# Input products of the state-space branch one projection later, and the pooling branch's running sums on GpSimd

## The chip, the cores and the metric

The kernel runs on one core of a Trainium2 chip. The metric is the device time of one execution in microseconds (us); less is better. The program of one core has five engines with an instruction queue each: TensorE (PE in the profile), VectorE (DVE), ScalarE (ACT), GpSimd (POOL) and SyncE (SP), which here issues the DMAs. An engine starts its instructions in the order of its queue; engines wait for each other by semaphores.

## The reference, cut to what matters

The reference is a network of two blocks on 512 tokens of 1024 channels in fp32. The change lies in the second block, whose first product is split into six parts; two branches work on them:

```python
h = _rmsnorm(x, norm_g[l])
proj = h @ w_in[l] + b_in[l]
ua, za, ub, zb, ga, gb = jnp.split(proj, SPLITS, axis=-1)
ya = _s5_branch(ua, ...) * jax.nn.silu(za)
yb = _pool_branch(ub, pool_w[l], pool_scale[l]) * jax.nn.silu(zb)
merged = jax.nn.sigmoid(ga) * (ya @ w_branch_a[l]) + jax.nn.sigmoid(gb) * (yb @ w_branch_b[l])
x = x + merged @ w_out[l]

def _s5_branch(u, ...):                 # 32 groups of 16 channels
    bu_re = jnp.einsum('blgc,gpc->blgp', ug, bbar_re)      # input products
    bu_im = jnp.einsum('blgc,gpc->blgp', ug, bbar_im)
    _, _, s_re, s_im = lax.associative_scan(_complex_linear_combine, (a_re, a_im, bu_re, bu_im), axis=1)
    y = einsum(s_re, c_re) - einsum(s_im, c_im) + d_skip * u
    ...

def _pool_branch(u, w_group, scale):    # 4 groups of 128 channels, a window for each
    mean = (csg - shifted) / count      # mean of the last `win` tokens
    outs.append(mean - u32[group])
    ...
    return einsum(pooled, w_group) * scale
```

## The kernel before

Tokens lie on the free axis: a tile is 128 channels by 512 tokens. A projection (`proj`) is one such tile: 24 matmuls of 128x512 into a PSUM tile `psp`, three (leading by leading, remaining by leading, leading by remaining parts of fp32 values, L264 to L266) for each of eight 128-channel slices k0 to k7, then one ScalarE instruction that adds the bias and applies the function. `chunk` calls a hook after each slice, so other matmuls can be put between the slices. Weights come as blocks of 128x1024 by DMA (`r_win`), one block for a projection here; ScalarE makes the leading part (`h_win`, L245) and VectorE the remaining part (`l_win`, L246).

The second block's projections come in this order, with what stands between them: ua0 to ua3; ub0, zb0, ub1, zb1, the pooling product out0, ub2, zb2, out1, ub3, zb3, za0, za1, out2, za2, out3, za3; then the gates. TensorE's order is written out by hand (`manual_schedule`); the order of the other engines is set by a scheduler from the program and its dependencies.

The state-space branch is a generator, `ssm_main`, that the program advances by `next(ssm)` or hands to `proj` as the hook. It loads tables, the input weights `wi` and the input `U` (written by ua0 to ua3 to DRAM and read back by eight DMAs, L1652). Then come the input products `pb`: eight groups of eight matmuls of 128x64 (L1658) in two halves each, with a step of the hook behind each half, and the copies to `BR` and `BI` on ScalarE (L1662, L1663). Behind the last of them VectorE runs a chain of 16 instructions: six products of `cmul` (L1371 to L1376) and two scans (L1668), four more products (L1672, L1673), four that write `XR` and `XI` (L1676). This chain is called the chain below. Two of the four output weight tiles `wo` reuse the chain's scratch buffers `bt0` and `bt1`, so their DMAs (L1681) wait for its end; the output products `py` (L1692, L1693) stand as the hook in za2 and za3 and need the first `wo` tile, `XR` and `XI`. With nine `yield`s in front of the input products, zb1's hook runs the eight groups.

The pooling branch is `pool_proj` (ub and zb), `pool_mix` (on VectorE: the running sum by doublings, 1 to 4 of them (L1732, each with a small copy, L1733), the product with the reciprocal counts `rcn` (L1736), the difference (L1737), then the split of the mean into `ybh` on ScalarE, L260, and `ybl` on VectorE, L261) and `pool_out` (three matmuls, scale and gate `ybf`, L1746, split again).

Of the kernel before, what the change touches and what calls it, by code (L numbers as in the profile page):

```python
# [11 lines left out]
AF = mybir.ActivationFunctionType  # L12
ALU = mybir.AluOpType
# [23 lines left out]
# x1 projections of the hyena mixer by the quarter of the channels that they follow  # L37
# [18 lines left out]
def host_inputs(inp):  # L56
# [68 lines left out]
    def both(a):  # L125
        # states on partitions twice, groups on the free axis; halves of the groups on partitions
        a = a.reshape(2, 16, 64)
        st = a.reshape(32, 64).T
        return np.concatenate([np.concatenate([st, st], axis=0), a.transpose(0, 2, 1).reshape(128, 16)], axis=1)
# [64 lines left out]
def build(nc, tc, A, dbg=None):  # L194
# [36 lines left out]
    class Stream:  # L231
        """128x128 weight units in blocks of eight, split into leading and remaining significand parts"""
# [85 lines left out]
    def residual_gemm(pp, ws, acts, evac, u_of=lambda m: m * 8, klead=2, nhalf=2, nxt=None, norm=None, at={}, bg=None, pss=None):  # L318
        if nhalf:
            nhalf, sk = NHS[ncall[0]], SKS[ncall[0]]  # L320
            ncall[0] += 1
        if callable(acts):
            n = KT
        else:
            n, acts = len(acts), acts.__getitem__

        def done(m, sl, ps):
            evac(m, sl, ps)
            if norm is not None:
                norm.add(m, sl)  # L330
            if bg is not None:
                bg(m)

        if pss is not None:
            klead = len(pss)
        else:
            pss = [pp.tile([128, L], F32, name="ps_r", tag="mm") for _ in range(klead)]
            for k in range(n):
                if k in at:
                    at[k]()  # L340
                for m in range(klead):
                    mm3(pss[m], ws.unit(u_of(m) + k), acts(k), k == 0, k == n - 1)
        acts = [acts(k) for k in range(n)]
        for m in range(klead):
            done(m, FULL, pss[m])
        if callable(pp):
            pp = pp()
        for m in range(klead, KT - nhalf):
            ps = pp.tile([128, L], F32, name="ps_r", tag="mm")
            chunk(ps, ws, u_of(m), acts, FULL)  # L350
            done(m, FULL, ps)
        if not nhalf:
            return
        if nxt is not None:
            for b in range(u_of(KT - nhalf) // 8, (u_of(KT - 1) + n - 1) // 8 + 1):
                ws.load(b)
            for b in range(3):
                nxt.load(b)
        # the table of the coming square roots, out of the way of the norm
        tc.keep_in_program_order(act.activation(dummy, epst, AF.Sqrt))  # L360
        for i, sl in enumerate(norm.parts):
            for m in range(KT - nhalf, KT):
                ps = pp.tile([128, L], F32, name="ps_r", tag="mm")[:, :sl.stop - sl.start]
                if i == 1 and m == KT - nhalf:
                    chunk(ps, ws, u_of(m), acts, sl, at_steps({sk[0]: lambda: norm.stat(0), sk[1]: lambda: norm.spread(0)} if norm.hook() is None else {2: lambda: norm.stat(0)}))
                else:
                    chunk(ps, ws, u_of(m), acts, sl, norm.hook() if i == 1 and m == KT - 1 else None)
                done(m, sl, ps)
        if norm.hook() is None:
            norm.apply(0)  # L370

# [26 lines left out]
    # leading and remaining parts of both vectors as four stationary columns  # L398
# [27 lines left out]
    def range_sin(tp, out, a, shape, quarter=False, tag=""):  # L426
        """out = sin(a) (cos(a) if quarter) of an unbounded argument"""
# [18 lines left out]
    def hyena_filter(hp, tp, pp, t):  # L446
# [19 lines left out]
        # the layer's leading and remaining parts over each other: both times the weights' leading parts in one pass  # L466
# [33 lines left out]
        def spectrum(qd, m, ta):  # L500
            s = 1 - m
            # sums and differences of the residue classes (cosine parts for the sum sequence, sine for the other)
# [72 lines left out]
    def mod_cols(hf, nr, scr):  # L575
        """rows to columns, with the bias; gains of the norms"""
        pst = pp.tile([128, 16], F32, name="pst0", tag="mm")
        for n in range(8):
            pe.matmul(pst[:, 2 * n:2 * n + 2], scr[n // 4][:, (n % 4) * 128:(n % 4 + 1) * 128], sel if nr == 4 else ident[0:2, 0:2], start=True, stop=True)
        pv = pst.rearrange("p (j n s) -> p j s n", j=2, s=2)  # L580
        o = slice(4 * hf, 4 * hf + 4)
        for s_, g in ((0, gM0), (1, gC0)):
            d = scc[:, 8 * s_ + 4 * hf:8 * s_ + 4 * hf + 4]
            dve.tensor_tensor(out=d, in0=pv[:, 1, s_], in1=V("modb", 8 + 4 * hf, 4), op=ALU.add)
            gain(g[:, o], d, V("nmix", 4 * hf, 4))
        for s_, dst in ((0, mods[:, o]), (1, shc[:, o])):
            dve.tensor_tensor(out=dst, in0=pv[:, 0, s_], in1=V("modb", 4 * hf, 4), op=ALU.add)
# [21 lines left out]
    def rstat_of(acc, dim, ps=None):  # L609
        """1/rms over the channels, on the tokens' partitions"""  # L610
# [9 lines left out]
    def rspread(sd, ps=None, out=None):  # L620
        """back to the free axis, the same on every partition"""
# [278 lines left out]
    # the queries' norm goes with the rotary table, token by token  # L900
# [27 lines left out]
    def osplit(k):  # L928
        """remaining parts in place of the previous head pair's values"""
# [5 lines left out]
    def wo_lead():  # L935
        """first output tiles, as far as the heads are done"""
# [87 lines left out]
    class Norm:  # L1024
        """rms norm of the residual stream: statistics as its tiles get ready, use in halves of the tokens"""
# [25 lines left out]
        def stat(self, i):  # L1051
            """on the tokens' partitions"""
# [20 lines left out]
        def spread(self, i):  # L1073
            """back to the free axis, the same on every partition"""
# [122 lines left out]
    up = Stream(A["wup"][1], "up1")  # L1197

    def hyena(ws, hh, hl, pre, norm, nxt):
# [15 lines left out]
        # convolution constants: interior bias, corrections at the two ends  # L1215
# [19 lines left out]
        def fft(q, vh, vl):  # L1235
            """transform, product with the filter's spectrum and inverse butterflies of 256 channels"""
            hf, cs = q // 2, slice((q % 2) * W, (q % 2) * W + W)
            # pairs of real and imaginary parts; (im, re) where they are combined crosswise
# [145 lines left out]
    def ssm_prep(ph):  # L1384
        """weights of the state-space branch for chunks of T steps"""
# [5 lines left out]
        # columns of the small tables: all groups, states' real parts over imaginary ones; then halves of the groups  # L1391
# [4 lines left out]
        # imaginary parts have the opposite sign on the lower half of the stacked tables  # L1396
# [21 lines left out]
        # powers of the transition  # L1418
# [19 lines left out]
        # input coefficient times the powers, for steps that lie 0..7 before the chunk's last  # L1438
# [9 lines left out]
        # the skip connection is a diagonal part of the kernel's tap of lag zero (its rows are the last sixteen)  # L1448
# [13 lines left out]
        def weights(name, q, a, b, x, op):  # L1462
            """a x + b y or a x - b y of complex numbers, real parts over imaginary ones"""
# [16 lines left out]
        for q in range(4):  # L1480
            gs = slice(8 * q, 8 * q + 8)
            # kernel taps
# [13 lines left out]
            # input weights, transposed  # L1496
# [12 lines left out]
            # output weights: real part and negated imaginary part of C abar^(t+1)  # L1509
# [12 lines left out]
        # conjugate powers of the phasor of T steps, decay of T steps  # L1522
# [34 lines left out]
    # final norm of the first block and the second block's norm in one pass over the statistics  # L1557
# [4 lines left out]
    # 1/rms of the once normed stream, without the first norm's factor: the sum of squares of x sqrt(g^2 + eps)  # L1562
# [74 lines left out]
    def ssm_main(pa):  # L1637
# [15 lines left out]
        for _ in range(9):  # L1653
            yield
# [14 lines left out]
        # back to the states' own phase: multiply by the conjugate table; real over imaginary parts  # L1669
# [47 lines left out]
    def pool_proj(gi, hook=None):  # L1717
# [3 lines left out]
        proj(12 + gi, AF.Silu, zb, hook)  # L1721
        ubz[gi] = (ub, zb)

    def pool_mix(gi):
# [4 lines left out]
        for s in range(gi + 1):  # L1729
            w = 1 << s  # L1730
            nxt = tmp("cum")
            dve.tensor_tensor(out=nxt[:, w:], in0=run[:, w:], in1=run[:, :L - w], op=ALU.add)  # L1732
            dve.tensor_copy(nxt[:, :w], run[:, :w])  # L1733
            run = nxt
        mean = tmp("mean")
        dve.tensor_tensor(out=mean, in0=run, in1=rcn, op=ALU.mult)  # L1736
        dve.tensor_tensor(out=mean, in0=mean, in1=ub, op=ALU.subtract)  # L1737
# [18 lines left out]
    pool_proj(1, ssm)  # L1756
    pool_out(0)
    pool_mix(1)
    next(ssm)
    pool_proj(2)  # L1760
# [36 lines left out]
    # gated linear unit of the state-space branch  # L1797
# [23 lines left out]
    # gated sum of the branches  # L1821
# [25 lines left out]
    class Final(Norm):  # L1847
        """last norm: tokens to the partitions, where the statistics scale them"""
# [84 lines left out]
```

## Time and profile before

| | us |
|---|---|
| median of 3 runs | 1738.53 |
| lowest and highest | 1736.77, 1740.84 |
| span of the profiled execution | 1744.6 |
| PE busy in it | 1718.7 (99%) |
| DVE busy | 1223.3 (70%) |
| ACT busy | 840.1 (48%) |
| POOL busy | 0.7 (0%), 9 instructions |

The profiled execution is 6.1 us longer than the median. Sums are made on its own times, and their difference is laid on the median. "Busy" counts an engine's instructions, not its waits. A busy PE may run at a lower clock: the column PEclk of the views by stretch is the granted TensorE clock, 1.00 for 2.4 GHz and 0.50 for 1.2 GHz.

### The profile page before, as it was taken

The page shows a single profiled execution, that of the slowest core. Times are in us where ns is not written, and L with a number is a line of the kernel's source. Part 1 is how long each engine was busy: PE and PEld are TensorE (multiplying, and loading weights), DVE is VectorE, ACT ScalarE, POOL GpSimd, SP SyncE. Part 2 cuts the span into 40 slices and gives each one's busy share as a digit, 9 for nine tenths or more (in the row PEclk, how much of TensorE's full clock was granted, in tenths as well). Part 3 has the DMA queues.
Part 4 walks back from the last instruction along what each step waited for, and adds up shares of the span by engine and source line. Part 5 has one row for each costly group of instructions (what it writes and reads, how often), then busy time and mean ns, then how long its engine had stood idle before and what let it go on. Part 6 is the DMA issues. An engine that isn't in the chain of part 4 may idle for free.

```text
span 1744.6 us, 22561 instructions
## 1 busy us (share of the span) xinstructions
PE 1718.7 (99%) x8645; PEld 1427.1 (82%) x8645; DVE 1223.3 (70%) x2065; ACT 840.1 (48%) x1299; POOL 0.7 (0%) x9
## 2 busy tenths in 40 slices
PE   8999999999999999999999999999999999999998
PEld 2678888887988888888888898888888898888887
DVE  5666999884799875654899969884586452927443
ACT  4566889995544313433533355442244243345234
POOL 0000000000000000000000000000000000000000
PEclk8989999999999999999999999999999997999999
DMA  6533432111478773222332332444542246443221
GB/s 226 185 132 115 139 109 91 37 37 61 153 237 270 266 244 109 97 99 84 122 105 97 113 109 79 146 138 150 141 145 97 97 166 143 150 116 121 97 85 49
DMA packets 91862, 224.87 MB, mean 129 GB/s; under 512 B 22728, under 2 KB 38344, under 8 KB 91626
## 3 DMA queue, kind: packets, MB, share of 16 engines
q1 hardware_dynamic: 91754, 223.42, 38.8%
q8 instruction: 68, 1.11, 0.3%
q14 instruction: 40, 0.33, 0.1%
HBM read 206.64 MB, written 16.74 MB: 128 GB/s over the span
## 4 chain that ended last, share of the span: by engine, by line
PE 90%; DVE 5%; ACT 2%; DMA 1%; issue 1%; SPq 0%; DVEq 0%
PE ps_r L264 7%; PE ps_r L265 7%; PE ps_r L266 7%; PE psg L266 4%; PE psg L265 4%; PE psg L264 4%; PE psa L266 4%; PE psa L264 4%; PE psa L265 4%; PE psp L264 3%; PE psp L265 3%; PE psp L266 3%; PE pac L498 2%; PE pst L880 2%; PE pso L891 1%
## 5 line engine op out<-in xcount | busy, mean ns | idle before, releaser
L245 ACT ACTIVATE h_up<-r_up 128x1024 fp32r<-128x1024 f32 x88 | 92.9, 1056 | 146.9 <-PE psg L265 81.3
L264 PE MATMUL ps_r<-mh,h_dn 128*128 128x512 f32 (+1 forms) x407 | 148.5, 365 | 0.0
L265 PE MATMUL ps_r<-ml,h_dn 128*128 128x512 f32 (+1 forms) x407 | 148.3, 364 | 0.0
L266 PE MATMUL ps_r<-mh,l_dn 128*128 128x512 f32 (+1 forms) x407 | 148.3, 364 | 0.0
L246 DVE TENSOR_TENSOR l_up<-r_up,h_up 128x1024 fp32r<-128x1024 f32 x88 | 107.4, 1220 | 52.0 <-ACT h_up L245 47.3
L266 PE MATMUL psg<-hh,l_up 128*128 128x512 f32 x336 | 132.9, 396 | 0.0
L265 PE MATMUL psg<-hl,h_up 128*128 128x512 f32 x336 | 131.7, 392 | 0.0
L264 PE MATMUL psg<-hh,h_up 128*128 128x512 f32 x336 | 131.5, 391 | 0.0
L266 PE MATMUL psa<-hh,l_up 128*128 128x512 f32 x320 | 125.9, 394 | 0.0
L265 PE MATMUL psa<-hl,h_up 128*128 128x512 f32 x320 | 124.6, 389 | 0.0
L264 PE MATMUL psa<-hh,h_up 128*128 128x512 f32 x320 | 124.5, 389 | 0.0
L386 DVE CUSTOM_DVE_ANT_0 mr<-mr,cb 128x1024 f32<-128x1024 f32 x80 | 97.0, 1218 | 23.1 <-DMA mr<-modT 22.4
L245 ACT ACTIVATE h_dn<-r_dn 128x1024 fp32r<-128x1024 f32 x44 | 46.5, 1057 | 105.4 <-PE ps_r L265 65.1
L264 PE MATMUL psp<-hh,h_win 128*128 128x512 f32 x232 | 94.5, 407 | 0.0
L265 PE MATMUL psp<-hl,h_win 128*128 128x512 f32 x232 | 91.8, 396 | 0.0
L266 PE MATMUL psp<-hh,l_win 128*128 128x512 f32 x232 | 91.8, 396 | 0.0
L246 DVE TENSOR_TENSOR l_dn<-r_dn,h_dn 128x1024 fp32r<-128x1024 f32 x44 | 53.6, 1221 | 49.6 <-ACT h_dn L245 49.6
L265 PEld LDWEIGHTS ps_r<-ml,h_dn 128*128 128x128 f32 x407 | 76.5, 188 | 13.6
L264 PEld LDWEIGHTS ps_r<-mh,h_dn 128*128 128x128 f32 x407 | 76.5, 188 | 13.6
L266 PEld LDWEIGHTS ps_r<-mh,l_dn 128*128 128x128 f32 x407 | 76.5, 188 | 13.6
L246 DVE TENSOR_TENSOR l_win<-r_win,h_win 128x1024 fp32r<-128x1024 f32 x32 | 39.0, 1223 | 67.9 <-ACT h_win L245 67.7
L1156 ACT ACTIVATE og<-og 128x512 f32<-128x512 f32 x44 | 27.8, 631 | 111.8 <-DVE og L1113 110.1
(663 smaller groups left out, 4598.4 us busy)
## 6 DMA issues: line engine op xcount, KB each, us to landing
r_up<-wup SPq DMA_DIRECT2D x88, 512.0 KB, 3.7
mr<-modT SPq DMA_DIRECT2D x80, 512.0 KB, 4.3
r_dn<-wdn SPq DMA_DIRECT2D x44, 512.0 KB, 3.7
r_win<-win SPq DMA_DIRECT2D x32, 512.0 KB, 3.4
r_hyin<-hyin SPq DMA_DIRECT2D x24, 512.0 KB, 3.3
rmod<-mod SPq DMA_DIRECT2D x8, 512.0 KB, 6.6
x<-xT SPq DMA_DIRECT2D x16, 256.0 KB, 4.8
Hd<-ho SPq DMA_DIRECT2D x16, 256.0 KB, 2.3
```

Of the source, the lines that this page charges most:

```text
L245: act.activation(hi, raw, AF.Copy)
L246: dve.tensor_tensor(out=lo, in0=raw, in1=hi.bitcast(F32), op=ALU.subtract)
L264: pe.matmul(ps, w[0], a[0], start=start, stop=False)
L265: pe.matmul(ps, w[0], a[1], start=False, stop=False)
L266: pe.matmul(ps, w[1], a[0], start=False, stop=stop)
L386: dve.tensor_tensor_reduce(raw, raw, cb, 1.0, 0.0, ALU.mult, ALU.add, mods[:, n:n + 1])
L498: pe.matmul(ps, tabs[:, o * 128:(o + 1) * 128], ta[r], start=(i == 0), stop=(i == len(terms) - 1))
L880: pe.transpose(pst[:, i * 128:(i + 1) * 128], Pt[h, i][:, j * 128:(j + 1) * 128], ident)
L891: pe.matmul(Ot[h], vw, pth, start=(j == 0), stop=False)
L1156: act.activation(og, og, AF.Silu)
```

## The change

Comment lines that only went away are left out. `ssm_main` yields once instead of nine times before the input products; `zb` projections no longer run the hook, and the hook goes with projection ub2 instead of ub1 and zb1. The running sums, their small copies, the product with `rcn` and the difference go from VectorE to GpSimd: 18 instructions of 128 by about 512 and 10 small copies (3 and 1 in the first mix, 4 and 2, 5 and 3, 6 and 4 in the others). The split of the mean stays on ScalarE and VectorE. Lines behind L1653 have a number less by one afterwards.

```diff
@@ ssm_main
-        for _ in range(9):
-            yield
+        yield
         for q in range(4):
             pb = pp.tile([128, 8, NJ], F32, name="pb", tag="bg", bufs=2)
@@ pool_proj
         proj(8 + gi, AF.Identity, ub, hook)
-        proj(12 + gi, AF.Silu, zb, hook)
+        proj(12 + gi, AF.Silu, zb)
@@ pool_mix
             nxt = tmp("cum")
-            dve.tensor_tensor(out=nxt[:, w:], in0=run[:, w:], in1=run[:, :L - w], op=ALU.add)
-            dve.tensor_copy(nxt[:, :w], run[:, :w])
+            nc.gpsimd.tensor_tensor(out=nxt[:, w:], in0=run[:, w:], in1=run[:, :L - w], op=ALU.add)
+            nc.gpsimd.tensor_copy(nxt[:, :w], run[:, :w])
             run = nxt
         mean = tmp("mean")
-        dve.tensor_tensor(out=mean, in0=run, in1=rcn, op=ALU.mult)
-        dve.tensor_tensor(out=mean, in0=mean, in1=ub, op=ALU.subtract)
+        nc.gpsimd.tensor_tensor(out=mean, in0=run, in1=rcn, op=ALU.mult)
+        nc.gpsimd.tensor_tensor(out=mean, in0=mean, in1=ub, op=ALU.subtract)
@@ order of the second block
     pool_mix(0)
-    pool_proj(1, ssm)
+    pool_proj(1)
     pool_out(0)
     pool_mix(1)
+    pool_proj(2, ssm)
     next(ssm)
-    pool_proj(2)
     next(ssm)
     pool_out(1)
```

On TensorE, before, the input products stand in projection zb1 (weight block 7), from behind its first slice on:

```order
L264 MATMUL psp<-hh_9545,h_win_7_13129 128x512
L265 MATMUL psp<-hl_9553,h_win_7_13129 128x512
L266 MATMUL psp<-hh_9545,l_win_7_13130 128x512
L1658 MATMUL pb<-U,wi 128x64 x4
L264 MATMUL psp<-hh_9546,h_win_7_13129 128x512
L265 MATMUL psp<-hl_9554,h_win_7_13129 128x512
L266 MATMUL psp<-hh_9546,l_win_7_13130 128x512
L1658 MATMUL pb<-U,wi 128x64 x4
```

Now they stand in ub2 (weight block 8), behind zb1 and the three matmuls of out0 (`ybh_13010` and `pwl` are its last):

```order
L266 MATMUL psp<-ybh_13010,pwl 128x512
L264 MATMUL psp<-hh_9545,h_win_8_13161 128x512
L265 MATMUL psp<-hl_9553,h_win_8_13161 128x512
L266 MATMUL psp<-hh_9545,l_win_8_13162 128x512
L1657 MATMUL pb<-U,wi 128x64 x4
L264 MATMUL psp<-hh_9546,h_win_8_13161 128x512
L265 MATMUL psp<-hl_9554,h_win_8_13161 128x512
L266 MATMUL psp<-hh_9546,l_win_8_13162 128x512
L1657 MATMUL pb<-U,wi 128x64 x4
```

So the products ask for `U` one projection and out0 later in the program.

On VectorE, before, the beginning of the chain (`bt`, `XR`) stands between the instructions of the second mix (`ybl_13015` is its `ybl`):

```order
L1732 TENSOR_TENSOR cum<-ub 128x511
L1733 COPY cum<-ub 128x1
L1371 TENSOR_TENSOR bt_13257<-BR,TR__13023 128x1024
L261 TENSOR_TENSOR ybl_13014<-ybf,ybh_13010 128x512
L1732 TENSOR_TENSOR cum<-cum 128x510
L1733 COPY cum<-cum 128x2
L1372 TENSOR_TENSOR bt_13258<-BI,TI__13024 128x1024
L1736 TENSOR_TENSOR mean<-cum,rcn 128x512
L1373 TENSOR_TENSOR XR<-bt_13257,bt_13258 128x1024
L1737 TENSOR_TENSOR mean<-mean,ub 128x512
```

Now the second half of the chain on VectorE holds the `ybl` of the third and fourth mix (`ybl_13016`, `ybl_13017`), whose means GpSimd makes, and the remaining part of the weights of za2 (`l_win_14`) stands behind it:

```order
L1671 TENSOR_TENSOR bt_13323<-BR,TR__13023 128x1024
L1672 TENSOR_TENSOR bt_13324<-BI,TI__13024 128x1024
L261 TENSOR_TENSOR ybl_13015<-ybf,ybh_13011 128x512
L1675 TENSOR_TENSOR XR<-bt_13323,bt_13324 64x1024
L1675 TENSOR_TENSOR XI<-bt_13323,bt_13324 64x1024
L261 TENSOR_TENSOR ybl_13016<-mean,ybh_13012 128x512
L1671 TENSOR_TENSOR bt_13323<-BI,TR__13023 128x1024
L1672 TENSOR_TENSOR bt_13324<-BR,TI__13024 128x1024
L261 TENSOR_TENSOR ybl_13017<-mean,ybh_13013 128x512
L1675 TENSOR_TENSOR XR<-bt_13323,bt_13324 64x1024
L1675 TENSOR_TENSOR XI<-bt_13323,bt_13324 64x1024
L246 TENSOR_TENSOR l_win_14_13506<-r_win_14_13503,h_win_14_13505 128x1024
```

No running sum is left on VectorE there, and the chain's last instructions come after two that read what GpSimd writes.

On GpSimd, which had nine memsets, the fourth mix now reads:

```order
L1731 TENSOR_TENSOR cum<-ub 128x511
L1732 COPY cum<-ub 128x1
L1731 TENSOR_TENSOR cum<-cum 128x510
L1732 COPY cum<-cum 128x2
L1731 TENSOR_TENSOR cum<-cum 128x508
L1732 COPY cum<-cum 128x4
L1731 TENSOR_TENSOR cum<-cum 128x504
L1732 COPY cum<-cum 128x8
L1735 TENSOR_TENSOR mean<-cum,rcn 128x512
L1736 TENSOR_TENSOR mean<-mean,ub 128x512
```

It is the last of the four, which stand in GpSimd's queue one behind the other.

## Rows read from the trace of the kernel before

**Rows 1.** The page: its head and its first part, busy time by engine.

```profile
span 1744.6 us, 22561 instructions
PE 1718.7 (99%) x8645; PEld 1427.1 (82%) x8645; DVE 1223.3 (70%) x2065; ACT 840.1 (48%) x1299; POOL 0.7 (0%) x9
```

**Rows 2.** Waits of PE, 1440 to 1550 us: total us, times, longest.

```profile
PE pb L1658 <- DMA r_win<-win: 2.8, 1, 2.8
PE psp L264 <- ACT ybh L260: 1.1, 1, 1.1
```

**Rows 3.** By stretch: us; busy PE, PEld, DVE, ACT, POOL; PEclk, DMA share, GB/s.

```profile
1458.20:1461.10 2.90, 0.10 (x1) 0.00 (x0) 0.00 (x0) 0.14 (x1) 0.00 (x0) 0.98 1.04 299
1461.10:1482.70 21.60, 21.56 (x86) 19.67 (x86) 1.23 (x1) 5.44 (x8) 0.00 (x0) 0.53 0.17 65
1482.70:1489.10 6.40, 6.40 (x30) 5.29 (x30) 6.14 (x10) 2.94 (x6) 0.00 (x0) 1.00 0.26 87
1489.10:1516.80 27.70, 27.70 (x123) 22.73 (x122) 27.55 (x30) 6.78 (x9) 0.00 (x0) 1.00 0.37 126
1516.80:1519.40 2.60, 1.25 (x5) 0.67 (x4) 2.47 (x5) 1.21 (x2) 0.00 (x0) 1.00 0.97 254
```

**Rows 4.** PE in order of time: start, us, instruction, times, idle before and releaser.

```profile
1461.14 1.94 PE L1658 MATMUL pb<-U,wi 128*128 128x64 f32 x8 [2.84 <-DMA r_win<-win]
...
1481.85 1.00 PE L1658 MATMUL pb<-U,wi 128*128 128x64 f32 x8
1482.66 0.48 PE L264 MATMUL psp<-ybh,pwh 128*128 128x512 f32 x1
...
1520.10 0.33 PE L1692 MATMUL py<-U,wk 128*128 128x64 f32 x2
```

**Rows 5.** SP's DMA issues in order of time: start, us, line, transfer, times.

```profile
1447.09 7.54 SPq L1652 DMA_DIRECT2D U<-Ud  x8
...
1512.39 0.80 SPq L1681 DMA_DIRECT2D wo<-Wod  x2
```

**Rows 6.** DVE in order of time, 1485 to 1512 us: parts of the chain.

```profile
1485.43 1.22 DVE L1371 TENSOR_TENSOR bt<-BR,TR__13023 128x1024 f32<-128x1024 f32 x1
1486.56 0.69 DVE L261 TENSOR_TENSOR ybl<-ybf,ybh 128x512 fp32r<-128x512 f32 x1
1487.16 0.68 DVE L1732 TENSOR_TENSOR cum<-cum 128x510 f32<-128x510 f32 x1
...
1494.18 2.29 DVE L1668 TENSOR_TENSOR_SCAN BR<-R__13025,XR 128x1024 f32<-128x1024 f32 x1
...
1497.50 0.75 DVE L1746 SCALAR_TENSOR_TENSOR ybf<-psp,vecs,zb 128x512 f32<-128x512 f32 x1
...
1509.87 1.22 DVE L1676 TENSOR_TENSOR XR<-bt,bt 64x1024 f32<-64x1024 f32 x1
1511.11 1.22 DVE L1676 TENSOR_TENSOR XI<-bt,bt 64x1024 f32<-64x1024 f32 x1
```

**Rows 7.** DMA by transfer, 1505 to 1520 us: KB each, median us to landing.

```profile
wo<-Wod SPq DMA_DIRECT2D x4, 512.0 KB, 4.1
```

**Rows 8.** ACT in order of time, 1480 to 1490 us: one instruction.

```profile
1489.98 0.69 ACT L1621 ACTIVATE ub<-psp,vecs 128x512 f32<-128x512 f32 x1
```

**Rows 9.** POOL in order of time: two of its nine instructions.

```profile
0.73 0.21 POOL L217 MEMSET ones<- 128x128 f32 x1 [0.29 <-POOLq L1923]
0.87 0.10 POOL L218 MEMSET epst<- 128x1 f32 x1
```

**Rows 10.** By stretch, columns as in rows 3, around two other stalls.

```profile
432.00:434.00 2.00, 0.20 (x1) 0.20 (x2) 0.90 (x2) 1.00 (x2) 0.00 (x0) 1.00 0.00 0
434.00:436.00 2.00, 2.00 (x9) 1.52 (x9) 1.18 (x2) 0.94 (x1) 0.00 (x0) 1.00 0.00 0
...
164.00:166.00 2.00, 0.96 (x8) 0.72 (x6) 1.34 (x3) 0.86 (x2) 0.00 (x0) 1.00 0.30 88
168.00:170.00 2.00, 2.00 (x11) 2.00 (x11) 1.72 (x5) 1.09 (x4) 0.00 (x0) 0.50 0.82 315
```

## The prediction

> **What bounds the kernel now.** I read the page first: PE is busy for 1718.7 of 1744.6 us, DVE for 1223.3 and POOL for 0.7 [rows 1], so a change pays only where PE waits or runs slowly. The view of PE's waits between 1440 and 1550 us names two that matter: 2.8 us of the input products pb, and 1.1 us of out2 for ybh [rows 2]. The first stall is larger than its own length. The view by stretch [rows 3] has PE idle from 1458.2 to 1461.1, and then 21.6 us at a granted clock of 0.53, nearly all of it at the lower of the two levels (1.2 GHz), although PE has work all the time; from 1482.7 on it is 1.00 again. The releaser printed for pb is the DMA of r_win, but that is only the transfer that came last by the profile; pb reads U, whose eight DMAs take 7.54 us to issue, until 1454.6 [rows 5], and the matmul that waits is pb's [rows 4]. I take U as the cause.
>
> Behind that, DVE is the engine to watch: from 1489.1 to 1516.8 us it is busy for 27.55 of 27.70 [rows 3], with the chain between the running sums [rows 6]. Out2 and py come right behind it: py starts at 1520.10 [rows 4].
>
> **Part 1, the products one projection later: PE's side.** Costs at the full clock: 123 matmuls of 128x512 in 27.70 us [rows 3] are 0.225 each, so a projection is 5.4 and a pooling product 0.7. Eight pb matmuls take 0.81, from 1481.85 to the next start at 1482.66 [rows 4], so all 64 take 6.5, and a projection with them 11.9.
>
> In the new order PE goes on at 1458.2 with the 21 matmuls left of zb1 (4.7, to 1462.9), out0 (to 1463.6) and ub2 with pb (11.9, to 1475.5). pb asks for U at 1464.3, some 3 us after it was there before (1461.14, [rows 4]); the same DMAs stand in the same place of SP's queue, ahead of r_win, with only the load of rcn moved up behind them. So this wait is gone. With it goes the low clock: 21.6 us were 11.9 of work, 9.7 lost. Ub2 ends at 1475.5 instead of 1489.1: PE is 13.6 us earlier. The five projections and out1 behind it (27.70) end at 1503.2; out2 and the first slice of za2 need 0.7 each, so py is reached at 1504.6 if nothing waits.
>
> **The chain's side.** It started 2.77 us after pb's end (1482.66 to 1485.43, [rows 4, 6]); now pb ends at 1475.5, so it starts at 1478.3, only 7.2 earlier, because the products were put later by what the stall had cost. Its length, from start to start: a product 1.13 and a split 0.60 (1485.43, 1486.56, 1487.16), a scan 2.20 (2.29 with the same overlap of 0.09), XR or XI 1.24 [rows 6]. Ten products, two scans and four of these make 11.3 + 4.4 + 5.0 = 20.7. By the new order three ybl (1.8) and one ybf (0.7) stand among them: 23.2 of DVE's own. Alone, it ends at 1501.5; the wo transfers behind it were issued at 1512.39, right at its end (1511.11 + 1.22), and take 4.1 to land [rows 5 to 7], which gives 1505.6. That is 1.0 after PE asks, and 14.5 before 1520.10. This is the best the change can do: **−14.5**, with no slack.
>
> **Part 2, the sums on POOL: what they cost.** DVE is rid of 18 instructions of 128x512 at 0.60 and 10 copies, about 12 us, of which most lay in or near the chain; the 23.2 already has them out. What they take on POOL no row shows, since POOL runs nine memsets. Lower bound: the 0.69 that DVE takes for a split of this size [rows 6]. Upper bound: a memset of 128x128 holds POOL for 0.14 (0.73 to 0.87, [rows 9]), so 128x512 would be 0.56, and two reads and a write three times that, 1.7. I take the middle, 1.2; for a copy of 1 to 8 columns 0.1 (a memset of 128x1, [rows 9]) to 0.25, taken as 0.2.
>
> Mixes 0 and 1 are covered: the first has from ub0 to out0, some 13 us of PE's work, for 3.8, and the second has ub2 and zb2 for 5.2. Mix 2 can start when ub2 is evacuated, 1.6 after PE's end (1489.1 to 1489.98 + 0.69, [rows 3, 8]), at 1477.1, and mix 3 when ub3 is, at 1488.7. Both run beside the chain: 11 large and 7 small instructions, 11 x 1.2 + 7 x 0.2 = 14.6 us. If the engines don't disturb each other, mix 2 ends at 1483.7 and mix 3 at 1496.7, before the ybl that read them come up (the last one 3.1 before the chain's end, at 1498.4), and the chain waits for nothing; at 1.7 it would wait some 2.
>
> **The step that decides.** How much of these 14.6 us falls on the chain, by slower instructions or by waits, no row can tell, since DVE and POOL never work together before. The bounds are none and all; below none is excluded, as the chain's 23.2 can't shrink. What each amount D is worth: py is late by D over 1505.6, and PE's wait grows to 1.0 + D in all. A wait of 2.84 us was followed by the low clock [rows 4, 3], one of 1.8 us at 432 was not, and one around 165 was for some us only [rows 10]; out2's stop before (1.25 busy of 2.60, rows 3) did nothing to the clock either. So for D up to about 2 the gain stays at 12 or more; from about 2 on the low clock under the products py, which mix with projection matmuls as pb did, gives back up to 9.7. Only the lowest tenth or so of the possible D gives a faster kernel. I therefore take the far end, all of it: the two engines take turns, D = 14.6 + 0.6 (the ScalarE copy of the last mean, which the last ybl then waits for as well) = 15.2. The chain ends at 1516.7 and wo lands at 1520.8. Behind the chain in DVE's queue stands the l_win of za2, so PE waits in pieces: some 3 us before out2 (ybl of mix 2), and some 12 more between out2 and py.
>
> The Trainium skill, page "SBUF — State Buffer", section "SBUF: two separate sides", says that a VectorE instruction with two SBUF inputs and a GpSimd instruction that reads SBUF exclude each other for a whole instruction. No run here shows it yet; by it the sum is the one with turns, and without it the one of the best case. The page "GPSIMD Engine Reference", section 3.1, measured an add at 4497 ns on GpSimd against 2293 on VectorE; scaled from the 0.69 of this trace I estimate 1.35 a piece from it, which would make the turns 1.7 us longer.
>
> **Sum.** py at 1520.8 against 1520.10 is +0.7; the low clock costs +9.7, as in the stretch of 21.6. In sum +10.4: the profiled execution would be 1755.0, and since it is 6.1 above the median, the median **1748.9**. With 0.69 a piece and 0.1 a copy, D is 8.9: −14.5 + 8.9 + 9.7 = +4.1, 1742.6; with 1.7 and 0.25, D is 21.0: +16.2, 1754.7.
>
> **The rivals.**
> 1. *Not slower: the engines run side by side.* DVE's instructions of one kind have equal length whatever ACT and PE do beside them (1.22 at 1485 and 1511, [rows 6]), which speaks for it; that a two-operand instruction on POOL needs the same memory speaks against. D is 0 to 2, the clock stays: −14.5 to −12, 1724 to 1727. It decides up to D of 2. Chance 0.20.
> 2. *Partly disturbed:* D between 2 and 6, or turns with the clock kept. −12.5 to −8.5, with 9.7 given back or less; or +0.7 with no loss of clock. 1734 to 1742. Chance 0.13.
> 3. *Turns, and dearer:* POOL nearer 1.7, or the low clock through za2 and za3, which both carry py (two times 9.7 instead of one). 1738.5 + 0.7 + 19.4 = 1758.6; with both 1764. Chance 0.17.
> 4. *The change doesn't do what it says:* pb waits for U in its new place, or something else (the first instruction on POOL, late rcn) stops PE there for 3 us, so the low clock comes back at pb and what is won is lost. About 1738. Chance 0.03.
> The forecast, turns at 0.69 to 1.7 with one stretch of low clock, 1742 to 1755, has 0.47.
>
> **How the numbers follow.** About 0.2%, 3.5 us, is what a measurement of this kernel can tell from no change. Faster than 1735: rival 1 (0.20) and a third of rival 2 (0.04), 0.24. Within 1735 to 1742: the rest of rival 2, rival 4 and the edge of the forecast, 0.13. Slower: 0.63. The range reaches over the upper half of rival 1 and most of rival 3: 1726 to 1760.
>
> **What would show it.** In the profile after: no wait of pb and PEclk 1.00 in zb1, out0 and ub2 (part 1); the chain's start some 7 us earlier than 1485.43; POOL rows of 0.7 to 1.7 us for the large instructions; then, for the forecast, chain instructions or POOL instructions that are longer, or start later, where both engines work, an end of the chain at about 1517, waits of PE for ybl, l_win and wo of 15 us together, and a stretch of PEclk near 0.5 under py. I am wrong if the chain ends before about 1504, with instructions of 1.22 beside a busy POOL, or if PE waits long before py and its clock stays at 1.00.

## The result, and the profile after

The changed kernel took 1754.74 us (median of 5 runs, 1751.27 to 1766.60) where the kernel before took 1738.53 (median of 5 runs taken beside them, 1736.27 to 1743.80). The ratio is 1.0104, with a 95% interval of 1.0075 to 1.0133: slower by about 1%. The forecast was 1748.9, in a range of 1726 to 1760.

The page of the profiled execution (1766.6 us, the longest of the five): its head and its first part. The rows answer to [rows 1].

```profile
span 1764.7 us, 22576 instructions
PE 1734.4 (98%) x8645; PEld 1440.4 (82%) x8645; DVE 1218.7 (69%) x2037; ACT 839.2 (48%) x1299; POOL 37.9 (2%) x37
```

DVE's busy time fell by 4.6 us only, where 28 instructions less should take some 12 off it, and POOL's rose by 37.2, where the prediction had 24 (18 x 1.2 + 10 x 0.2). Both engines were busy longer than forecast.

PE's waits between 1440 and 1570 us (total, times, longest), which answer to [rows 2]:

```profile
PE psp L266 <- DVE l_win L246: 7.4, 1, 7.4
PE py L1692 <- DMA wo<-Wod: 1.4, 1, 1.4
```

Both waits of before are gone. pb no longer waits, and neither does out2. In their place PE waits 7.4 us for the l_win of za2 and 1.4 for the first wo, 8.8 in all where it was 4.1.

The same program by stretch, columns as in [rows 3]:

```profile
1458.20:1477.00 18.80, 18.80 (x118) 16.72 (x116) 4.56 (x6) 9.51 (x15) 4.92 (x6) 1.00 0.37 137
1477.00:1504.20 27.20, 27.20 (x122) 22.51 (x122) 26.74 (x17) 6.51 (x10) 23.81 (x16) 1.00 0.18 59
1504.20:1512.00 7.80, 2.13 (x10) 1.42 (x8) 4.62 (x5) 3.31 (x5) 4.24 (x3) 0.84 0.62 201
1512.00:1518.00 6.00, 2.87 (x10) 2.59 (x11) 5.21 (x6) 0.63 (x1) 0.00 (x0) 0.50 0.74 265
1518.00:1564.00 46.00, 46.00 (x169) 41.37 (x169) 6.24 (x7) 7.89 (x11) 0.00 (x0) 0.50 0.28 75
```

From zb1 to za1 (the first two rows) PE is busy all the time at 1.00, where before it stood for 2.9 us and ran at 0.53 for 21.6 [rows 3]. Then it stops, and from the stop on the clock is 0.50, for 46 us of work and more (some 57 us in all, to about 1567): in this execution the low clock has moved from the products pb to the products py, and it lasts more than twice as long.

Where the stop comes from stands in the rows of DVE and POOL in order of time (start, us, idle before and releaser). Two stretches of the chain, DVE first:

```profile
1478.57 1.87 DVE L1371 TENSOR_TENSOR bt<-BR,TR__13023 128x1024 f32<-128x1024 f32 x1
1480.36 1.21 DVE L1372 TENSOR_TENSOR bt<-BI,TI__13024 128x1024 f32<-128x1024 f32 x1
1481.61 1.94 DVE L1373 TENSOR_TENSOR XR<-bt,bt 128x1024 f32<-128x1024 f32 x1
...
1502.71 2.29 DVE L1671 TENSOR_TENSOR bt<-BI,TR__13023 128x1024 f32<-128x1024 f32 x1
1504.92 1.21 DVE L1672 TENSOR_TENSOR bt<-BR,TI__13024 128x1024 f32<-128x1024 f32 x1
1509.29 0.69 DVE L261 TENSOR_TENSOR ybl<-mean,ybh 128x512 fp32r<-128x512 f32 x1 [3.16 <-ACT ybh L260]
...
1511.23 1.22 DVE L1675 TENSOR_TENSOR XI<-bt,bt 64x1024 f32<-64x1024 f32 x1
1512.48 3.49 DVE L246 TENSOR_TENSOR l_win<-r_win,h_win 128x1024 fp32r<-128x1024 f32 x3
```

The last row is the l_win that PE waits for: it starts when the chain has ended. And POOL, three rows of mix 1, when DVE has little to do, then mix 2 beside the chain, and the first and last row of mix 3:

```profile
1460.64 0.19 POOL L1732 COPY cum<-ub 128x1 f32<-128x1 f32 x1
1460.91 1.04 POOL L1731 TENSOR_TENSOR cum<-cum 128x510 f32<-128x510 f32 x1
...
1462.16 1.28 POOL L1735 TENSOR_TENSOR mean<-cum,rcn 128x512 f32<-128x512 f32 x1
...
1479.31 1.18 POOL L1732 COPY cum<-ub 128x1 f32<-128x1 f32 x1
1480.57 1.91 POOL L1731 TENSOR_TENSOR cum<-cum 128x510 f32<-128x510 f32 x1
1482.42 1.18 POOL L1732 COPY cum<-cum 128x2 f32<-128x2 f32 x1
...
1494.15 1.15 POOL L1731 TENSOR_TENSOR cum<-ub 128x511 f32<-128x511 f32 x1 [1.83 <-ACT ub L1621]
...
1507.34 1.26 POOL L1736 TENSOR_TENSOR mean<-mean,ub 128x512 f32<-128x512 f32 x1
```

Alone, an add on POOL takes 1.04 us and a copy of one column 0.19. Beside the chain the add takes 1.91 and the copy 1.18. The copy is the telling row: it begins at 1479.31 in the middle of DVE's L1371 (1478.57 to 1480.44), and ends when that one has. The next add, recorded from 1480.57, spends its first microsecond beside L1372, which runs until 1481.57 at its usual 1.21; then the add finishes at 1482.48, and L1373, which started at 1481.61, stretches to 1.94. The chain runs from 1478.57 to 1512.45, 33.9 us, where DVE's own work in it is 23.2: nine of its instructions are longer (by 0.4 to 1.1, 7.1 in all), and 3.2 are a wait for the last mean; 0.4 are spread over the other starts. That mean is late because POOL is held up too: by the starts in mix 1 an add with its copy takes 1.25 us, the product 1.36 and the difference 1.30, so the ten instructions of mix 3 would take 7.7 us alone. Here they take 14.5 (1494.15 to 1508.60). In 7.7 they would have been done well before DVE came to the ybl that reads the mean, at 1506.13.

### The profile page after: what moved, and what is told of

The parts are those of the page before. It is cut to its first block, busy times and chain, and to the rows that moved or that the text cites. A ratio compares the mean times of both kernels' runs of the same rounds, so it can differ in the third digit from the quotient of the medians.

```text
span 1764.7 us, 22576 instructions
## 1 busy us (share of the span) xinstructions
PE 1734.4 (98%) x8645; PEld 1440.4 (82%) x8645; DVE 1218.7 (69%) x2037; ACT 839.2 (48%) x1299; POOL 37.9 (2%) x37
## 4 chain that ended last, share of the span: by engine, by line
PE 92%; DVE 3%; ACT 2%; DMA 1%; issue 1%; POOL 1%; SPq 0%; POOLq 0%; DVEq 0%; ACTq 0%
PE ps_r L264 7%; PE ps_r L265 7%; PE ps_r L266 7%; PE psg L266 4%; PE psg L265 4%; PE psg L264 4%; PE psa L266 4%; PE psa L265 4%; PE psa L264 4%; PE psp L264 4%; PE psp L265 4%; PE psp L266 4%; PE pac L498 2%; PE pst L880 2%; PE pso L891 1%; PE pso L892 1%
## 5 line engine op out<-in xcount | busy, mean ns | idle before, releaser
L246 DVE TENSOR_TENSOR l_win<-r_win,h_win 128x1024 fp32r<-128x1024 f32 x32 | 38.8, 1223 | 62.3 <-ACT h_win L245 62.2
```

What stands on the lines that cost most here:

```text
L246: dve.tensor_tensor(out=lo, in0=raw, in1=hi.bitcast(F32), op=ALU.subtract)
```

## The experiments

The theory was: **A**, GpSimd (POOL) and VectorE (DVE) take turns, so the sums lengthen the chain, and the move of pb is right in itself. Its rivals: **B**, the later place of the products alone makes py late; **C**, no turns, GpSimd is just slow and stands ahead of the chain in the order. Medians of all executions, beside the kernel before on the same chip:

| run | PE's waits in its profile, us | us, median (range, executions) | ratio to before (95%) | mean granted clock |
|---|---|---|---|---|
| changed kernel | 8.8 | 1754.74 (1751.27 to 1766.60, 5) | 1.0104 (1.0075, 1.0133) | 0.971 to 0.981 |
| e1: the move alone | 0.9 + 3.2 | 1739.10 (1736.68 to 1752.51, 10) | 1.0021 (0.9992, 1.0050) | 0.979 to 0.988 |
| e2: the sums alone | 2.4 + 5.4 | 1762.93 (1745.73 to 1771.12, 4) | 1.0133 (1.0058, 1.0209) | 0.969 to 0.985 |
| e3: no sums in mixes 2, 3 | 1.7 | 1733.51 (1730.88 to 1755.20, 10) | 0.9990 (0.9955, 1.0025) | 0.976 to 0.990 |
| e6: another order, sums on DVE | 0.9 | 1733.60 (1731.66 to 1735.68, 10) | 0.9974 (0.9951, 0.9997) | 0.987 to 0.990 |
| e6b: e6, mixes 0, 1 on POOL | 0 | 1731.70 (1729.26 to 1733.78, 10) | 0.9949 (0.9933, 0.9965) | 0.987 to 0.990 |
| e9: sums that nothing reads | 2.1 + 7.4 | 1765.56 (1764.27 to 1766.16, 4) | 1.0143 (1.0104, 1.0181) | 0.971 to 0.973 |
| e10: memsets | 0.9 | 1731.71 (1) | | 0.989 |
| e11: e6, all sums on POOL | 8.6 | 1765.99 (1764.60 to 1766.55, 4) | 1.0134 (1.0100, 1.0168) | 0.971 to 0.973 |

The kernel before, in the 25 executions beside e1 to e6, had a mean clock of 0.981 to 0.993, 0.988 in the median. Beside e6b, e9, e10 and b1 it had 0.981 to 0.990, with 1739.56 us and 0.987 in the median of 13, and beside e11, a2 and b2 0.982 to 0.989, with 1743.89 us and 0.984 in the median of 7. Span times one less that clock is what an execution loses to a low clock: 20.9 us at 0.988. In its first profile (0.982, 31 us lost) 19 us are lost in the first 200 us (0.86 and 0.95 in the two hundreds), which the change doesn't touch; in b1 it is 15 there.

**The move alone (e1).** Both hunks of the pooling sums undone:

```diff
-            nc.gpsimd.tensor_tensor(out=nxt[:, w:], in0=run[:, w:], in1=run[:, :L - w], op=ALU.add)
-            nc.gpsimd.tensor_copy(nxt[:, :w], run[:, :w])
+            dve.tensor_tensor(out=nxt[:, w:], in0=run[:, w:], in1=run[:, :L - w], op=ALU.add)
+            dve.tensor_copy(nxt[:, :w], run[:, :w])
...
-        nc.gpsimd.tensor_tensor(out=mean, in0=run, in1=rcn, op=ALU.mult)
-        nc.gpsimd.tensor_tensor(out=mean, in0=mean, in1=ub, op=ALU.subtract)
+        dve.tensor_tensor(out=mean, in0=run, in1=rcn, op=ALU.mult)
+        dve.tensor_tensor(out=mean, in0=mean, in1=ub, op=ALU.subtract)
```

> The change without its second part: the input products stand in ub2, the sums stay on VectorE. Theory A (GpSimd and VectorE take turns, which lengthens the chain; the move itself is right): pb does not wait, PEclk is 1.00 from zb1 to ub2, the chain starts at about 1478.6 as in the changed kernel and takes its own 20.7 plus one ybf, one ybl, one cum and one l_win, some 24 us instead of the 33.9 of the changed kernel, so it ends at about 1502.5 and wo lands at about 1506. Out2 then waits some 3 us for the third mix, which VectorE makes behind the chain; py starts at about 1509. 1728 if the clock stays, up to 1745 if these 3 us are enough to lower it under py. Rival B (the later place of the products alone makes py late, GpSimd is not the point): a chain as late as in the changed kernel, wo at about 1516, 1750 to 1765.

PE's waits of e1 in the same stretch (total, times, longest):

```profile
PE psp L264 <- ACT ybh L260: 3.2, 1, 3.2
PE pb L1657 <- ACT BI L1662: 0.9, 1, 0.9
```

The chain took 24.1 us (1480.02 to 1504.08) with products of 1.20 to 1.23; py waits for nothing, out2 waits 3.2 for its mean, as forecast. Rival B is out: 1739.10 is the time of the kernel before, within the interval. But the gain of 10 us that theory A allowed isn't there either, though seven of the ten executions have a mean clock of 0.986 to 0.988, about that of the kernel before in its median. That pointed at the other side of the comparison, the kernel before, and to the last experiment below.

**The sums alone (e2).** The changed `pool_mix` with the old order of calls, nine yields and the old hook.

> The change without its first part: the products stay in zb1, the sums go to GpSimd. Theory A: the stall of pb (2.8 us) and the low clock from 1461 to 1482 stay as before; from 1490 on mixes 2 and 3 on GpSimd run into the chain and lengthen it by some 10 us, to about 1520; wo lands at about 1524 and py waits some 6 us where out2 waited 1.4, so +4 at full clock, with a second low stretch under py +14 to +25: 1742 to 1765. Rival B: the sums on GpSimd cost nothing or free VectorE, 1736 to 1739.

```profile
PE psp L266 <- DVE l_win L246: 5.4, 1, 5.4
PE pb L1658 <- DMA r_win<-win: 2.4, 1, 2.4
```

The first row is PE's new wait, the second the old one. Behind the old one the clock fell in this execution as it had in the first profile of the kernel before; the row, with columns as in [rows 3]:

```profile
1459.20:1476.00 16.80, 16.80 (x64) 15.35 (x65) 1.23 (x1) 3.51 (x6) 2.84 (x4) 0.51 0.28 99
```

The chain runs from 1481.26 to 1513.25, and the last ybl, behind it, waits 4.9 for POOL's mean. So the sums cost without the move: +1.3%, though the four executions lie far apart (1745.73 to 1771.12). A second wait was added in this order that theory A had not priced: `rcn` of mixes 1 and 2 is late for POOL (7.5 and 2.5 us).

**No sums beside the chain (e3).** Sums, product and difference of mixes 2 and 3 are left out.

```diff
-        for s in range(gi + 1):
+        for s in range(gi + 1 if gi < 2 else 0):
...
+        if gi >= 2:
+            split(ybh[gi], ybl[gi], ub)
+            ubz[gi] = zb
+            return
```

> The changed kernel with the sums, the product and the difference of mixes 2 and 3 left out (the split takes ub itself), so nothing runs on GpSimd beside the chain. Theory A and its rival C (GpSimd's own price and the order, not turns): the chain takes 23.2 us plus one l_win, starts at 1478.6 and ends at about 1503, instructions of 1.22 throughout, py waits at most 2 us, the clock stays at 1.00: about 1725. Rival B: py still waits some 8 us and the clock falls, over 1745.

The chain's first and last instruction in e3:

```profile
1475.39 1.23 DVE L1371 TENSOR_TENSOR bt<-BR,TR__13023 128x1024 f32<-128x1024 f32 x1
...
1498.69 1.22 DVE L1675 TENSOR_TENSOR XI<-bt,bt 64x1024 f32<-64x1024 f32 x1
```

It takes 24.5 us, one l_win (1.2) more than the 23.2 of the prediction's sum; py waits 1.7 for wo (1.0 forecast), and the clock is 1.00 throughout in the profiled execution. The best case of the prediction is there as a sequence. As a time it is 1733.5, not 1725: 5 us under the kernel before in the median, not 14.5, and by the ratio's interval (0.9955 to 1.0025) not clear of no change, since two of the ten executions took 1745.25 and 1755.20. Against B it is decisive, between A and C it is not.

**Sums that nothing reads (e9), and memsets (e10).** In e9 GpSimd does the sums of mixes 2 and 3 as in the changed kernel, but the split takes ub as in e3. In e10 a copy of one column and 45 memsets, which read no tile, stand in their place (the split of ub is as in e3):

```diff
+            if gi == 2:
+                nxt = tmp("cum")
+                nc.gpsimd.tensor_copy(nxt[:, :1], ub[:, :1])
+                for s in range(45):
+                    nc.gpsimd.memset(nxt, 0.0)
```

> The run without sums (e3), but GpSimd does the sums of mixes 2 and 3 all the same, into tiles that nothing reads, so that no engine waits for them: the output leaves them out. Theory A (turns): the chain grows by what GpSimd holds beside it, 8 to 11 us over the 24.5 of e3, single VectorE instructions take 1.9 to 2.3 instead of 1.22 and GpSimd's copies 1.18 instead of 0.18; PE waits 5 to 8 us before py and the clock falls there in most executions: 1745 to 1765. Rival C (only GpSimd's price and the place of ybl in the order): the chain is 24.5 long as in e3, all instructions 1.22, 1731 to 1735.

> As e9, but GpSimd runs 45 memsets of 128x512 (no operand is read) beside the chain in place of the sums; the output leaves the sums of mixes 2 and 3 out. If reading is what the two engines take turns on, the chain has 1.22 a product and is 24.5 long, as in e3, and the time is 1731 to 1735; if any GpSimd instruction that touches the memory holds VectorE back, products take 1.5 to 1.9 and the chain is 10 to 20 us longer.

DVE and POOL of e9 in order of time, where no instruction of DVE reads what POOL writes:

```profile
1483.65 1.94 DVE L1374 TENSOR_TENSOR bt<-BR,TI__13024 128x1024 f32<-128x1024 f32 x1
1485.51 1.21 DVE L1375 TENSOR_TENSOR bt<-BI,TR__13023 128x1024 f32<-128x1024 f32 x1
1486.65 3.37 DVE L1667 TENSOR_TENSOR_SCAN BR<-R__13025,XR 128x1024 f32<-128x1024 f32 x1
...
1510.13 2.17 DVE L1675 TENSOR_TENSOR XI<-bt,bt 64x1024 f32<-64x1024 f32 x1
```

```profile
1484.46 1.18 POOL L1734 COPY cum<-cum 128x4 f32<-128x4 f32 x1
1485.72 2.15 POOL L1737 TENSOR_TENSOR mean<-cum,rcn 128x512 f32<-128x512 f32 x1
1487.95 3.16 POOL L1738 TENSOR_TENSOR mean<-mean,ub 128x512 f32<-128x512 f32 x1
```

and of e10, DVE's chain and POOL's memsets in one row:

```profile
1476.57 1.23 DVE L1371 TENSOR_TENSOR bt<-BR,TR__13023 128x1024 f32<-128x1024 f32 x1
1482.98 2.28 DVE L1667 TENSOR_TENSOR_SCAN BR<-R__13025,XR 128x1024 f32<-128x1024 f32 x1
...
1499.86 1.22 DVE L1675 TENSOR_TENSOR XI<-bt,bt 64x1024 f32<-64x1024 f32 x1
```

```profile
1476.57 26.22 POOL L1733 MEMSET cum<- 128x512 f32 x45
```

In e9 the chain takes 34.3 us (1478.03 to 1512.30) against 24.5 in e3, although no wait ties it to POOL: scans of 3.37 instead of 2.28, products of 1.94 instead of 1.22. In e10 it is 24.5 with POOL busy all the while. So the lengthening is neither an order nor a wait of the program; it is what GpSimd's copies, sums and products, which read SBUF, do to VectorE instructions with two operands there, and memsets, in the one execution of e10, don't; that the reads do it is inferred from the memsets, which only write. C is out as the cause of the long chain, and e9 alone, at 1765.56, costs at least as much as the changed kernel, a little over the 1745 to 1765 that was expected. The Trainium skill, page "SBUF — State Buffer", section "SBUF: two separate sides", states this exclusion for such pairs. The rows agree that the two exclude each other; that VectorE stands for the whole of GpSimd's instruction they do not show, since an add recorded as 1.04 alone cost it 0.65 to 0.84.

**Another order (e6), with mixes 0 and 1 on GpSimd (e6b), with all sums there (e11).** All three have pb in ub2, call `pool_mix(2)` ahead of the chain and put the first wo into a buffer that is free after the scans:

```diff
     pool_proj(2, ssm)
+    pool_mix(2)
     next(ssm)
...
-    pool_mix(2)
     pool_mix(3)
...
-            w = ap_.tile([128, 8, 128], F32, name="wo", tag=("bt0", "bt1", "TR_", "TI_")[i])
+            w = ap_.tile([128, 8, 128], F32, name="wo", tag=("R8_", "bt1", "TR_", "TI_")[i])
...
-            w = ap_.tile([128, 8, 128], F32, name="wk", tag=("wk", "R8_", "BR", "BI")[i])
+            w = ap_.tile([128, 8, 128], F32, name="wk", tag=("wk", "bt0", "BR", "BI")[i])
```

> The products in ub2, all sums on VectorE, mix 2 called ahead of the chain instead of behind it, and the first wo tile in the buffer of R8, which is free after the scans, so that its load no longer waits for the chain's end (the second wk takes the scratch buffer instead). Theory A: the chain with mix 2 in its first half starts at 1478.6 and ends at about 1504.5, l_win of za2 at about 1505.7, out2 does not wait, py starts at about 1506.3 and does not wait for a DMA; the clock stays at 1.00: 13 to 14 us faster than before, about 1725. Rival B: no gain over the kernel before, since the products' place makes py late; 1738 or more.

> As e6 (products in ub2, mix 2 ahead of the chain, first wo tile in R8's buffer), but mixes 0 and 1 stay on GpSimd, where VectorE has little to do. Theory A: GpSimd harms only beside a busy VectorE; both mixes end before the chain begins, the chain is as in e6, and the time equals e6 within 0.2%, 1731 to 1736. If GpSimd harms wherever it runs, 1740 or more.

> As e6 (products in ub2, mix 2 ahead of the chain, first wo tile in R8's buffer), with all sums on GpSimd: against e6b the engine of mixes 2 and 3 is the only difference in the code. Theory A (turns): mix 2 and mix 3 on GpSimd lengthen the chain by 7 to 11 us over the 24.5 of e3, although they relieve VectorE of 7 us of work; PE waits 3 to 8 us before py and the clock falls there in most executions: 1742 to 1765. If the loss of the changed kernel came from its order alone, 1730 to 1736 as e6b.

In e6 the chain takes 25.8 us with mix 2 in its first half, out2 and py wait for nothing, and the one wait left is 0.9 at pb. In e6b that one is gone too: PE waits for nothing between 1440 and 1600, and the ten executions lie within 4.5 us. Of the kernels that leave nothing out it has the lowest median, 0.5% under the kernel before, with an interval clear of no change. The forecast of 1725 for e6 was wrong by the same 9 us as for e3. That e6b is no slower than e6 shows that GpSimd does no harm where VectorE has little to do.

In e11, with the engine of mixes 2 and 3 as the only difference from e6b, PE waits 8.6 us and the time is 1765.99. The direction is the expected one, but each size lies above its range: the chain takes 38.8 us, 14.3 more than in e3 where 7 to 11 were expected, PE's wait is over 8 and the time over 1765. DVE in e11, in order of time:

```profile
1480.72 1.94 DVE L1373 TENSOR_TENSOR XR<-bt,bt 128x1024 f32<-128x1024 f32 x1
1487.41 0.69 DVE L261 TENSOR_TENSOR ybl<-mean,ybh 128x512 fp32r<-128x512 f32 x1 [4.74 <-ACT ybh L260]
1488.01 1.22 DVE L1374 TENSOR_TENSOR bt<-BR,TI__13024 128x1024 f32<-128x1024 f32 x1
...
1509.89 0.69 DVE L261 TENSOR_TENSOR ybl<-mean,ybh 128x512 fp32r<-128x512 f32 x1 [7.38 <-ACT ybh L260]
```

Three instructions are longer, by 2.1 together, and 12.1 us are waits: the two ybl stand earlier in the chain than in the changed kernel, and DVE stops until POOL has the mean. Two rows of POOL's mix 3 tell why it is so late:

```profile
1496.67 4.75 POOL L1731 TENSOR_TENSOR cum<-ub 128x511 f32<-128x511 f32 x1 [9.97 <-ACT ub L1621]
...
1502.64 1.04 POOL L1731 TENSOR_TENSOR cum<-cum 128x510 f32<-128x510 f32 x1
```

The first add is recorded with 4.75 us, beside five instructions of DVE of which only the last is longer: the turns do not alternate one by one here. From 1502.5 on DVE stands, and POOL is back at 1.04. By the 6.4 and 7.7 us that mixes 2 and 3 would take alone, where they take 9.6 and 12.5, some 8 of the 12.1 us come from turns that hold POOL up. Some 4 are left for rival C, GpSimd's own price and the place of the ybl; in the changed kernel nothing of the 3.2 needs it.

**More profiles of the two kernels (a2, b1, b2).** No edit.

> The kernel before once more, for a second profile. If the low clock under pb is a fixed price of its 2.8 us wait, PEclk is 0.5 for some 20 us from 1461 on again and the span is about 1744. If it follows that wait in some executions only, the stretch is shorter or missing, the mean clock is 0.987 to 0.991, and the span 1732 to 1737.

> The kernel before, a third profile: the wait of pb again 2.4 to 2.9 us; the low clock behind it either missing as in the second profile, or some us long. A time of 1733 to 1740 goes with a clock of 1.00 in most of pb's stretch.

> The changed kernel once more, for a second profile. Theory A: the chain again some 34 us long, with VectorE instructions of 1.9 to 2.3 beside GpSimd's, PE waits of 8 to 9 us in all before py; the low clock under py again, its length between 20 and 55 us, by which the executions of this kernel differ; 1751 to 1767.

By stretch, columns as in [rows 3]: the kernel before in b1, from the stall on:

```profile
1458.00:1461.00 3.00, 0.86 (x4) 0.38 (x2) 0.00 (x0) 0.69 (x1) 0.00 (x0) 1.00 1.08 192
1461.00:1464.00 3.00, 2.53 (x20) 2.43 (x20) 0.64 (x1) 1.06 (x1) 0.00 (x0) 1.00 0.90 358
1464.00:1474.00 10.00, 10.00 (x70) 9.14 (x69) 0.82 (x2) 4.85 (x8) 0.00 (x0) 1.00 0.23 79
```

The stall around 432 in b1, which left the clock at 1.00 in the first profile [rows 10]:

```profile
432.00:434.00 2.00, 1.21 (x3) 0.96 (x4) 0.77 (x2) 0.63 (x1) 0.00 (x0) 0.77 0.00 0
434.00:436.00 2.00, 2.00 (x6) 1.59 (x5) 0.89 (x2) 1.32 (x2) 0.00 (x0) 0.50 0.00 0
```

The changed kernel in a2:

```profile
1510.00:1520.00 10.00, 4.96 (x18) 4.39 (x19) 7.56 (x8) 2.85 (x5) 0.00 (x0) 0.50 0.78 294
1520.00:1530.00 10.00, 10.00 (x39) 9.04 (x39) 2.45 (x2) 2.71 (x3) 0.00 (x0) 0.50 0.45 149
1530.00:1540.00 10.00, 10.00 (x37) 8.94 (x36) 1.22 (x1) 2.23 (x3) 0.00 (x0) 0.50 0.08 13
1540.00:1550.00 10.00, 10.00 (x68) 9.11 (x68) 1.44 (x2) 1.23 (x2) 0.00 (x0) 0.97 0.39 64
```

In b1 pb waits 2.6 us, as in the profile that the prediction was read from (2.8), and PEclk stays at 1.00; so it does in b2, with a wait of 1.2, where 2.4 to 2.9 was expected. These executions took 1737.15 and 1733.78 us, at mean clocks of 0.990 and 0.989. The stretch of 21.6 us at 0.53 [rows 3] belongs to the execution that was profiled first, at a mean clock of 0.982. Which others carry it only their clocks can tell: of the 45 executions of the kernel before that ran beside the experiments, 17 lie at 0.985 or under, where 26 us or more are lost: 7 of 25, 5 of 13 and 5 of 7 in the three sets. So it is an estimate that the median one of the first two sets, at 0.988 and 0.987, has little of it; in the last set the median one may well have it. The wait at 432 (read as 1.8 us from its slice in the prediction) was 2.06 us in the first profile and in b1, and only in b1 did the clock fall. In a2 (1753.89 us) the waits are 7.4 and 1.0, DVE's chain is instruction for instruction that of the first profile, and the low clock lasts some 30 us, to about 1541, instead of some 57: by this the executions of the changed kernel differ.

## Why the prediction was right, point by point

- **PE's side of the move** held in its mechanism: no wait of pb, PEclk 1.00 from zb1 to ub2. That the chain starts at 1478.57 (forecast 1478.3) is two misses that cancel: pb ends at 1477.0 instead of 1475.5, and the chain follows 1.6 behind it instead of 2.8. PE reaches out2 at 1505.02, 1.8 later than forecast.
- **The low clock that the move takes away, −9.7**, was the mis-sized term of the first part. It is right for the execution that was profiled, and little for the median one, as far as b1, b2 and the clocks tell. The prediction took the 6.1 us by which the profile's span lay above the median time as a constant of the whole program (7.9, counted alike, since an execution's time is some 1.8 above its span in every run); this stretch alone is worth more than that. Counted from the first DMA of U to the first py, the kernel before takes 73.0 us in the first profile, but 63.3 in b1 and 61.7 in b2, and e6b takes 58.6. So for the median the best case was not −14.5: e3, where nothing but 1.7 us of wait is left, lies 5 lower in the median, and e6b 8.
- **The chain's own length** of 23.2 held (24.5 in e3 with one l_win more).
- **The price on POOL** (1.2 for a large instruction, 0.2 for a copy) was close: 1.04 for an add, 1.28 to 1.30 for the product and the difference, 0.19 for a copy.
- **All of it falls on the chain, D = 15.2**, had the right mechanism and was too large: 33.9 − 23.2 = 10.7. Taking turns costs DVE less than POOL's whole instruction: an add of 1.04 lengthens a product by 0.65 to 0.84, and a copy lengthens nothing that the rows show (L1372, behind the first copy, takes its usual 1.21). What POOL loses by the turns, which the prediction left out of its sum, makes the last mean late and comes back as the wait of 3.2.
- **PE's waits** came as l_win and wo, with 7.4 + 1.4 instead of 15; the first py that needs wo starts at 1516.25 instead of 1520.8; out2 did not wait, since mix 2 was done at 1492.3 and its ybl ran at 1502.1.
- **The low clock under py, +9.7**, was too small. It lasts 30 us (a2) to 57 us (first profile), which is the length that rival 3 had (through za2 and za3). At a clock of 0.979 the median execution loses 36.8 us to it in all where the kernel before loses 20.9 (at 0.988, beside e1 to e6; the clocks of the five executions beside the changed kernel are not on record): 16 us, of which some 3 pass while PE waits, so that 13 are a loss of their own.

In the median's own terms, as an estimate: the best case without the stretch at pb is −4.8 (−14.5 + 9.7), the chain gives back 10.7, the low clock costs 13: +19, where +16.2 was measured; the rest isn't accounted for, and some executions of the kernel before do carry a low stretch. The forecast came out 6 us low with the right sign because one gain that the median didn't have, a D too large by 4.5 and a clock too cheap by 3 to 6 stood against each other: the sign and the mechanism, turns, are earned, and the closeness of the number is partly luck. A fixed wait from which the loss begins, some 2 us in the prediction, is not what the runs show; they show a share of executions that grows with the wait. Of the kernels in the table whose profile shows waits up to 0.9 no execution fell under a clock of 0.987; at 1.7 two of ten did clearly, at 3.2 three of ten, and at 8.4 and more all did.

## What to carry to other kernels

An engine that seems free may not be free for the work that is moved to it, as GpSimd here for sums that read SBUF beside VectorE's two-operand instructions: look at what runs beside the moved work, and move it only to where the other engine rests, as mixes 0 and 1 of e6b. Count what both engines lose, the slower instructions of the one and the late results of the other. When a stretch at a low clock is read from one profile, look at the clocks of the other executions before it is put into a sum: it may be that execution's alone. And where a step is moved later in the program, its followers' slack is spent; an order that puts short work ahead of a long chain, and a buffer that lets the next load start early, gained 0.3% here (e6, with the later place of pb) where the move to the other engine lost 1%.

## What the runs showed of the hardware

GpSimd's instructions that read SBUF and VectorE's two-operand instructions shut each other out for a time: a copy of one column on GpSimd grew from 0.19 to 1.18 us, a product on VectorE from 1.22 to 1.94, a scan from 2.28 to 3.37 (e9), also where no data tie the two. GpSimd does not always get the next turn: an add waited beside four VectorE instructions in a row (e11, 4.75 us). Memsets on GpSimd (0.58 each, 26.22 us for 45) did nothing to VectorE's instructions (e10, one execution). VectorE's ybf, whose first operand lies in PSUM, ran in its usual 0.74 in the changed kernel beside the end of a difference on GpSimd; that is a single pair of rows.

The granted clock does not follow a wait in a fixed way: 2.6 us of idle PE left it at 1.00 in b1, 2.8 brought it to 0.53 for 21.6 us in the first profile of the same kernel, and 2.4 to 0.51 for 16.8 us in e2. The stall of 2.06 us at 432 did nothing to it in the first profile and halved it for some 3 us in b1. Behind waits of 8.4 us and more in all (the changed kernel, a2, e9, e11) it fell in all four profiles, to 0.50 for some 30 us in a2 and some 57 in the other three; the other ten executions of these kernels have mean clocks of 0.971 to 0.981, so it fell in them too. What sets this length stays open; none of these runs told it apart.
